# Ordering a weight copy behind the middle of an earlier weight slab, in a two-layer hybrid decoder kernel

## The chip, the core and the metric

The kernel runs on one core of one Trainium2 chip. The core has a matrix engine (TensorE, PE in the profile, with its weight loads as PEld), VectorE (DVE), ScalarE (ACT), GpSimd (POOL) and SyncE (SP, which here only issues transfers). Each engine takes its instructions from its own queue, in order. The metric is the device time of one execution in microseconds (us); the median of the runs counts.

## The reference

The reference computes two identical decoder layers on 512 tokens of width 1024, in float32. Each layer adds a block of four causal token mixers and then a SwiGLU feed-forward block:

```python
u = h @ w_in                       # one projection for all mixers and gates
y_a, y_b, y_c, y_d = fox(u), gla(u), retention(u), ssd(u)
merged = (g[:, :, 0] * (y_a @ w_up_a) + g[:, :, 1] * (y_b @ w_up_b)
          + g[:, :, 2] * (y_c @ w_up_c) + g[:, :, 3] * (y_d @ w_up_d))
x = x + merged @ w_out             # h = rms_norm(x, ln1)
gate, up = jnp.split(rms_norm(x, ln2) @ w_ffn_in, 2, axis=-1)
x = x + (jax.nn.silu(gate) * up) @ w_ffn_out    # 2816 hidden columns
```

Nearly all the arithmetic is in the products with weights. The weights are read once.

## The kernel before, in words

**Weights as slabs.** Every weight matrix is cut into blocks of 128 x 128. The order in which the program uses the blocks is written into the list `keys`, and eight blocks in a row make a slab (`SLAB = 8`, a tile of 128 x 1024 float32, 512 KB). There are 218 slabs in this stream, 109 per layer. `load()` (lines 247 to 253) allocates a raw tile `wr` (two buffers) and issues its transfer on SP's queue (line 252).

**High and low parts.** To keep float32 accuracy, each operand is split into a high part in the format float32r and the rest. `convert()` (lines 259 to 267) calls `split()` for a slab: line 214 is a ScalarE copy that writes the high part `wh`, and line 215 is a VectorE subtraction that writes the low part `wl`. Both have three buffers (the pool `wp`). A block times an activation tile is three matmuls, all issued in `mm` at line 200: high by high, high by low, low by high (`mm3`). So a usual slab is 24 matmuls of 512 columns. When the subtraction is done the raw tile is free and the next load into it can go.

**Who asks for a slab.** `block()` (lines 275 to 286) hands out one block after another. When it crosses into a slab it calls `ahead()`, which loads and converts up to `AHEAD = 2` slabs, so the conversion of slab n is written in the program at the first block of slab n-1. `wide()` (lines 288 to 297) hands out three slabs per layer in another shape and doesn't go through `block()`.

**Who sets the order.** The program is traced in this order, and a list scheduler with a timeline simulation then writes each engine's queue. It may move an instruction ahead of others when the simulated operands and buffers are there. Between engines there are semaphores for real dependences: a copy into `wh` waits for the transfer of `wr`, and for the last matmul of the slab that had the buffer before, which is slab n-3. `order(a, b)` (lines 226 and 227) adds an edge of class NoSync from instruction a to instruction b. Before the change its only use is in `act()`, where it keeps the loads of activation tables in their order on ScalarE.

**The stages of a layer.** First the projections with the mixers between them (`proj`, `group`; the mixers are generators, and weight products from the list `fill` are put between their steps), then `w_out` (lines 1207 to 1210), then the feed-forward block. This has a plain group of two hidden blocks and then four parts (`PARTS = (6, 6, 6, 4)`). In each part, `run()` computes hidden blocks with a Strassen scheme on its own stream of weights (`wsq`, loaded at lines 1274 and 1288 into `rq`, `wr` and `wl`, with high parts at lines 1295 and 214), and then the product with `w_ffn_out` takes slabs from the main stream: six per part, four in the last. Four output blocks are computed as a group, the others one by one, and each result is scaled and added to x on VectorE (lines 1424 and 1425). The loads of the Strassen stream share the two `wr` buffers and SP's queue with the slabs.

Of the kernel before, what the change touches and what calls it, by code (L numbers as in the profile page):

```python
# [35 lines left out]
SLAB = 8  # L36
# [98 lines left out]
def trunk(ctx: ExitStack, tc: tile.TileContext, keys, qkeys, xin, pos, wst, wsq, par, ext, cst, out):  # L135
    nc = tc.nc
    V, A, G, T = nc.vector, nc.scalar, nc.gpsimd, nc.tensor
# [20 lines left out]
    def piece(tag, shift=0):  # L158
        t = wp.tile([P, SLAB * P + 64], F32R, tag=tag, name=nm(tag))
        return t[:, shift:shift + SLAB * P]  # L160
# [36 lines left out]
        return ap.rearrange("p (c t) -> p c t", c=n)  # L197

    def mm(o, l, r, start, stop):
        T.matmul(o, lhsT=l, rhs=r, start=start, stop=stop, skip_group_check=True)  # L200

    def mm3(o, l, r, start, stop):
        (lh, ll), (rh, rl) = l, r
        mm(o, lh, rh, start, False)
        mm(o, lh, rl, False, False)
        mm(o, ll, rh, False, stop)
# [4 lines left out]
            mm(o, a, b, start and i == 0, stop and i == 1)  # L211

    def split(src, hi, lo):
        A.copy(out=hi, in_=src)  # L214
        V.tensor_tensor(out=lo, in0=src, in1=hi.bitcast(F32), op=ALU.subtract)  # L215
        return hi, lo

    def split_tile(t):
        return split(t, TT(F32R), TT(F32R))

    def split_small(t, shape, tag):
        return split(t, sp.tile(shape, F32R, tag=tag + "h", name=nm(tag), bufs=1), sp.tile(shape, F32R, tag=tag + "l", name=nm(tag), bufs=1))

    seen = {"set": None, "last": None}

    def order(a, b):
        tc.add_manual_dep(a.ins, b.ins.name, mybir.DependencyInfo(mybir.DependencyClass.NoSync, mybir.DependencyReason.DATA), reason="table")
# [13 lines left out]
            seen["last"] = i  # L241
        return i

    raw, ready = [], []
    cap = [SLABS]

    def load():
# [7 lines left out]
    def halves(n):  # L255
        w = SLAB * P
        return [slice(0, w // 2), slice(w // 2, w)] if n < 2 else [slice(0, w)]

    def convert():
        n = len(ready)  # L260
        if n < SLABS:
            far = n % (BLOCKS // SLAB) in TOKEN
            hi, lo = (piece("wh", 16), piece("wl", 48)) if far else (piece("wh"), piece("wl"))
            for h in halves(n):
                split(raw[n][:, h], hi[:, h], lo[:, h])
            ready.append((hi, lo))
            raw[n] = None

    def ahead(n):
        while len(ready) < min(SLABS, cap[0], n):  # L270
            if len(raw) == len(ready):
                load()
            convert()

    def block(*key, width=1):
        n = len(keys)
        if n % SLAB == 0:
            ahead(n // SLAB + AHEAD)
            if n // SLAB:
                ready[n // SLAB - 1] = None  # L280
        for i in range(width):
            keys.append(key[:-1] + (key[-1] + i * P,))
        i = n % SLAB
        hi, lo = ready[n // SLAB]
        sl = slice(i * P, (i + width) * P)
        return hi[:, sl], lo[:, sl]
# [141 lines left out]
    def group(name, l, cols, src, nk, hook=None):  # L428
        ps = [MX() for _ in cols]
        for k in range(nk):  # L430
            if hook and k == 4:
                hook()
            for i, c in enumerate(cols):
                mm3(ps[i], block(name, l, k, c), src[k], k == 0, k == nk - 1)
        return ps

    def proj(name, l, c, src, nk):
        ps = MM()
        for k in range(nk):
            mm3(ps, block(name, l, k, c), src[k], k == 0, k == nk - 1)  # L440
        return ps

    def layer(l, n1, scope):
# [72 lines left out]
        def tokmajor(dst, c, stacked=False):  # L516
            st = {}

            def go(half):
                def f():  # L520
                    if half == 0:
                        if not stacked:
                            dst.append(vp.tile([P, NB, 256], F32, tag="v", name=nm("v")))
                        st["ps"] = [MM(), MM()]
                    for k in range(4 * half, 4 * half + 4):
                        w = block("w_in", l, k, c, width=2)
                        assert (len(keys) - 1) // SLAB % (BLOCKS // SLAB) in TOKEN
                        for tb in range(NB):
                            ts = slice(tb * P, (tb + 1) * P)
                            o = st["ps"][tb // 2][:, (tb % 2) * 256:(tb % 2) * 256 + 256]  # L530
                            mm3(o, (n1.hi[:, k, ts], n1.lo[:, k, ts]), w, k == 0 and tb % 2 == 0, k == KD - 1)
                    if half:
                        for tb in range(NB):
                            v, rt = st["ps"][tb // 2][:, (tb % 2) * 256:(tb % 2) * 256 + 256], n1.rt[:, tb:tb + 1]
                            if stacked:
                                t = TT(F32R).rearrange("p (h s d) -> p h s d", h=NH, s=2)
                                v = v.rearrange("p (h d) -> p h d", h=NH)
                                act(out=t[:, :, 0], in_=v, func=AF.Copy, scale=rt)
                                V.scalar_tensor_tensor(out=t[:, :, 1], in0=v, scalar=rt, in1=t[:, :, 0].bitcast(F32), op0=ALU.mult, op1=ALU.subtract)
                                dst.append(t)  # L540
                            else:
                                act(out=dst[0][:, tb], in_=v, func=AF.Copy, scale=rt)
                return f
            return [(4.1, go(0)), (4.1, go(1))]
# [906 lines left out]
    o, w = PAR_OFF["ln1"]  # L1451
# [78 lines left out]
```

## Time and profile before

| What | Value |
|---|---|
| Runs | 1712.86, 1713.11 and 2853.69 us, median 1713.11 |
| The profiled execution's own time | 1713.04 us |
| Its span, first to last instruction | 1711.3 us |
| Granted TensorE clock | 1.000 |
| Busy: PE, PEld, DVE, ACT, POOL | 99%, 87%, 71%, 50%, 13% |
| Read from HBM, written | 191.28 MB, 2.10 MB |

The profile is a recording of one execution. Of a group of instructions it gives the line, the engine, the operation, the tiles written and read (without their numbers), the shapes and the count; after the bar stand the busy time and the mean of one in ns, and then the idle time of the engine just before them with what ended it. A row of the timeline is: start, length, engine, line, operation, tiles, shapes, count, and in brackets the idle time before it and what ended that. A row of the waits is: engine and line that waited, for whom, microseconds in total, times, the longest. A piece of the chain is: start, length, engine, tiles and line, count. `PE mm L200` is a matmul into a PSUM tile named mm, `mx` one of the other four PSUM banks. The ends of matmuls are modelled and overlap the next start, so their pace is read from starts.

### The profile page before, as it was taken

To read this page: it belongs to the slowest core of one execution; us is meant where nothing else is said; L and a number is where in the kernel's file an instruction comes from. 1 tells how busy PE (TensorE), PEld (TensorE's weight loads), DVE (VectorE), ACT (ScalarE), POOL (GpSimd) and SP (SyncE) were. 2 spreads that over 40 slices of the span, in tenths; PEclk is the share of its full clock that TensorE was granted. 3 is DMA by queue.
4 is the path that set the end of the run, shared out by engine and by line. 5 is a ranking of instruction groups with operands and counts; after the bars stand their busy time and mean duration, and the time that the engine had idled before them with its cause. 6 is when DMAs were issued, how large, how long until landed. Compare 5 with 4: busy or idle time off the path is not lost.

```text
span 1711.3 us, 25115 instructions
## 1 busy us (share of the span) xinstructions
PE 1700.9 (99%) x10124; PEld 1480.5 (87%) x10124; DVE 1210.9 (71%) x1693; ACT 863.5 (50%) x1194; POOL 216.4 (13%) x221
## 2 busy tenths in 40 slices
PE   9999999999999999999999999999999999999998
PEld 7878888888888999998988788888888889999997
DVE  6867666768677677675777666767776677767666
ACT  5425543546347646464544354435554474655643
POOL 3021210022101010101020212200221010101010
PEclk9999999999999999999999999999999999999999
DMA  5322222222235657575333222222222265665653
GB/s 200 106 74 74 75 86 75 86 87 74 85 110 142 194 132 188 136 185 120 91 98 111 74 74 74 87 76 94 77 87 87 99 171 163 153 174 139 177 115 106
DMA packets 54693, 195.00 MB, mean 114 GB/s; under 512 B 6064, under 2 KB 6448, under 8 KB 54576
## 3 DMA queue, kind: packets, MB, share of 16 engines
q1 hardware_dynamic: 45072, 160.45, 29.0%
q0 software_dynamic: 8640, 31.46, 10.3%
q8 instruction: 79, 1.29, 0.3%
q10 hardware_dynamic: 864, 1.48, 0.2%
q14 instruction: 38, 0.31, 0.1%
HBM read 191.28 MB, written 2.10 MB: 113 GB/s over the span
## 4 chain that ended last, share of the span: by engine, by line
PE 97%; DVE 1%; DMA 1%; ACT 1%; issue 0%; SPq 0%; DVEq 0%
PE mm L200 65%; PE mx L200 31%; PE mx L1080 1%; DMA x<-in_x_dram 0%; DMA wr<-in_wst_dram 0%; ACT wh L214 0%; DVE wl L215 0%; PE mx L693 0%; DVE t L371 0%; ACT L233 0%; ACT g L238 0%; DVE t L1169 0%; PE mx L952 0%; PE mx L872 0%; DVE n L409 0%
## 5 line engine op out<-in xcount | busy, mean ns | idle before, releaser
L214 ACT CAST wh<-wr 128x1024 fp32r<-128x1024 f32 (+1 forms) x240 | 250.1, 1043 | 367.8 <-PE mm L200 224.8
L200 PE MATMUL mm<-xh,wh 128*128 128x512 f32 (+1 forms) x1184 | 428.5, 362 | 0.9 <-DVE t L1169 0.9
L200 PE MATMUL mm<-xh,wl 128*128 128x512 f32 (+1 forms) x1184 | 427.9, 361 | 0.0
L200 PE MATMUL mm<-xl,wh 128*128 128x512 f32 (+1 forms) x1184 | 427.3, 361 | 0.0
L215 DVE TENSOR_TENSOR wl<-wr,wh 128x1024 fp32r<-128x1024 f32 (+1 forms) x220 | 285.5, 1299 | 118.4 <-ACT wh L214 116.0
L200 PEld LDWEIGHTS mm<-xh,wh 128*128 128x128 f32 x1184 | 222.4, 188 | 35.1 <-DVE t L1169 1.8
L200 PEld LDWEIGHTS mm<-xh,wl 128*128 128x128 f32 x1184 | 222.5, 188 | 34.6 <-issue 1.3
L200 PEld LDWEIGHTS mm<-xl,wh 128*128 128x128 f32 x1184 | 222.4, 188 | 33.9 <-issue 1.3
L200 PE MATMUL mm<-t,wh 128*128 128x512 f32 x448 | 140.2, 392 | 0.0
L200 PE MATMUL mx<-xl,wh 128*128 128x256 f32 (+1 forms) x448 | 138.3, 309 | 0.0
L200 PE MATMUL mx<-xh,wh 128*128 128x256 f32 (+1 forms) x448 | 136.0, 311 | 2.2 <-ACT wh L214 2.2
L1288 POOL DMA_DIRECT2D wl<-in_wsq_dram x60 | 51.9, 865 | 517.7 <-ACT wl L1287 368.1
L200 PE MATMUL mx<-f,wh 128*128 128x512 f32 x352 | 108.2, 390 | 0.0
L200 PE MATMUL mm<-f,wh 128*128 128x512 f32 x352 | 105.9, 389 | 0.0
L200 PEld LDWEIGHTS mm<-t,wh 128*128 128x128 f32 x448 | 83.2, 188 | 17.1
L215 DVE TENSOR_TENSOR l<-rq,wh 128x1024 fp32r<-128x1024 f32 x60 | 73.2, 1220 | 33.1 <-ACT wh L214 18.7
L200 PEld LDWEIGHTS mx<-xh,wh 128*128 128x128 f32 x448 | 84.0, 188 | 8.5 <-ACT wh L214 3.3
L200 PE MATMUL mx<-xh,wl 128*128 128x256 f32 (+1 forms) x288 | 91.0, 327 | 0.0
L200 PEld LDWEIGHTS mx<-xl,wh 128*128 128x128 f32 x448 | 84.1, 188 | 5.1
L200 PE MATMUL mm<-t,wl 128*128 128x512 f32 x224 | 87.4, 390 | 0.0
L214 ACT CAST wh<-rq 128x1024 fp32r<-128x1024 f32 x60 | 63.0, 1050 | 43.8 <-PE mm L200 21.5
L200 PEld LDWEIGHTS mm<-f,wh 128*128 128x128 f32 x352 | 66.1, 188 | 13.5
(280 smaller groups left out, 3438.1 us busy)
## 6 DMA issues: line engine op xcount, KB each, us to landing
wr<-in_wst_dram SPq DMA_DIRECT2D x216, 512.0 KB, 3.5
rq<-in_wsq_dram SPq DMA_DIRECT2D x60, 512.0 KB, 5.5
wl<-in_wsq_dram POOLq DMA_DIRECT2D x60, 512.0 KB, 7.3
wr<-in_wsq_dram SPq DMA_DIRECT2D x20, 512.0 KB, 6.9
out_dram<-x SPq DMA_DIRECT2D x8, 256.0 KB, 2.0
x<-in_x_dram SPq DMA_DIRECT2D x3, 512.0 KB, 6.5
wr<-in_wst_dram SPq DMA_DIRECT2D x4, 256.0 KB, 5.5
x<-in_x_dram SPq DMA_DIRECT2D x2, 256.0 KB, 4.6
```

The lines of the kernel that those rows point to most:

```text
L200: T.matmul(o, lhsT=l, rhs=r, start=start, stop=stop, skip_group_check=True)
L214: A.copy(out=hi, in_=src)
L215: V.tensor_tensor(out=lo, in0=src, in1=hi.bitcast(F32), op=ALU.subtract)
L1080: T.transpose(ps[:, W:W + P], zs[qb][:, kb * P:(kb + 1) * P], ident)
L1288: G.dma_start(out=lo, in_=wsq[j], accum_op=ALU.add)
```

## The change

`mm` and `split` now remember the last matmul and the last high-part copy that were traced. When `block()` hands out the fifth block of a slab (`i == SLAB // 2`), the last matmul traced before it, the third of the fourth block, is kept as that slab's middle. After each `split` in `convert()`, if slab n-2 has a middle, the copy of slab n gets an edge to it by `order()`.

```diff
     def mm(o, l, r, start, stop):
-        T.matmul(o, lhsT=l, rhs=r, start=start, stop=stop, skip_group_check=True)
+        seen["mm"] = T.matmul(o, lhsT=l, rhs=r, start=start, stop=stop, skip_group_check=True)
...
     def split(src, hi, lo):
-        A.copy(out=hi, in_=src)
+        seen["copy"] = A.copy(out=hi, in_=src)
...
-    raw, ready = [], []
+    raw, ready, middle = [], [], {}
...
                 split(raw[n][:, h], hi[:, h], lo[:, h])
+                if n - 2 in middle:
+                    order(seen["copy"], middle[n - 2])
...
         i = n % SLAB
+        if i == SLAB // 2:
+            middle[n // SLAB] = seen["mm"]
         hi, lo = ready[n // SLAB]
```

No operand, shape, buffer or transfer changes.

## The prediction

> **What bounds the kernel now.** I read the page first, then whom TensorE (PE) waited for, then the chain of work that ended last, for PE's pace, then the waits and the timeline of ScalarE (ACT), on which the changed instruction runs.
>
> ```profile
> span 1711.3 us, 25115 instructions
> ...
> PE 1700.9 (99%) x10124; PEld 1480.5 (87%) x10124; DVE 1210.9 (71%) x1693; ACT 863.5 (50%) x1194; POOL 216.4 (13%) x221
> ```
> ```profile
> PE mx L200 <- ACT wh L214: 2.2, 3, 1.1
> PE mm L200 <- POOL t L327: 1.4, 1, 1.4
> PE mx L200 <- DVE t L215: 1.2, 2, 0.7
> PE mm L200 <- DVE t L1169: 0.9, 2, 0.5
> ```
>
> PE is busy for 1700.9 of 1711.3 us, and all recorded waits of PE come to 2.2 + 1.4 + 1.2 + 0.9 = 5.7 us. Of these the first two rows belong to the start (warm-up, and the first three slabs); in the middle of the kernel PE waits 2.1 us in all. No other engine's idle time can be worth more than this, so a gain has a floor close by. A loss has none.
>
> Busy records overlap, so a busy PE could still be a slow one. Its pace is in the pieces of the chain (start, length, what):
>
> ```profile
> 503.10 21.76 PE mm L200 x96
> 585.92 16.34 PE mx L200 x72
> 602.27 19.12 PE mm L200 x96
> 621.39 2.72 PE mx L200 x24
> 1434.47 16.34 PE mx L200 x72
> 1450.82 19.12 PE mm L200 x96
> 1469.94 2.72 PE mx L200 x24
> ```
>
> In the first row 96 matmuls of 512 columns, which are four slabs, take 21.76 us: 226.7 ns each, 5.44 us for a slab of 24, 2.72 us for half a slab.
>
> **What the change does, part by part.** It adds no instruction and no byte. It adds an ordering edge from the ScalarE copy of slab n's high part (line 214, called by convert) to the last matmul before the fifth block of slab n-2. The edge is of class NoSync: I take it as an order for the list scheduler that writes the queues, without a semaphore, so on the chip the copy still waits only for its load and for its buffer. What changes is where it stands in ScalarE's queue. In the code 210 of 218 slabs get an edge: not the first two, and not the slab two behind each of the six that wide() consumes, since those never pass through block().
>
> (1) The copy. Its rows on the page, and ScalarE's own waits:
>
> ```profile
> L214 ACT CAST wh<-wr 128x1024 fp32r<-128x1024 f32 (+1 forms) x240 | 250.1, 1043 | 367.8 <-PE mm L200 224.8
> ...
> L215 DVE TENSOR_TENSOR wl<-wr,wh 128x1024 fp32r<-128x1024 f32 (+1 forms) x220 | 285.5, 1299 | 118.4 <-ACT wh L214 116.0
> ```
> ```profile
> ACT wh L214 <- PE mm L200: 246.3, 95, 7.5
> ```
> ```profile
> 519.23 1.06 ACT L214 CAST wh<-wr 128x1024 fp32r<-128x1024 f32 x1 [3.24 <-PE mm L200]
> ```
>
> In this row of the steady stage a copy has stood at the head of ScalarE's queue for 3.24 us, until a matmul freed its buffer. There are three buffers, so that matmul was the last of slab n-3: the copy starts as slab n-2 begins, and slab n begins two slabs later: 2 x 5.44 = 10.88 us, less 1.05 for the copy, leaves 9.83 us of cover. Half a slab later 9.83 - 2.72 = 7.11 us are left. Cost on PE: 0, hidden by the one and a half slabs of matmuls still to run. Without that cover each late microsecond would be one of PE.
>
> What stands behind the copy goes up to 2.72 us sooner, and the 246.3 us in 95 waits (2.6 us each, near the 2.72 that the copy moves) should fall by more than half. I value this at 0, because PE waits 2.2 us for that engine, at the start. Its upper bound is the 2.1 us of waits in mid-kernel.
>
> (2) The subtraction behind it (line 215 on VectorE, 1.30 us mean) moves as far: 9.83 - 1.30 = 8.53 us of cover become 5.81. In VectorE's queue it stood with 116.0 us of waits for the copy; behind it stand PSUM evacuations, for which PE waited 0.9 us in all.
>
> (3) The loads. SP's queue holds the load of slab n+2 behind that subtraction:
>
> ```profile
> SPq L252 <- DVE wl L215: 954.1, 176, 12.1
> ```
> ```profile
> wr<-in_wst_dram SPq DMA_DIRECT2D x216, 512.0 KB, 3.5
> ```
>
> Copy 1.05, subtraction 1.30 and landing 3.5 make 5.85 us from one copy to the data of the copy two slabs on, against 10.88 us: 5 us to spare, unchanged, since both ends move together. Cost 0. The Strassen loads (line 1274) that share SP's queue come at most 2.72 us later. POOL's queue isn't passed.
>
> (4) The ends of the feed-forward parts, the tightest place. There the raw buffers are shared with Strassen tiles, and the sixth slab of a part can be loaded only when the fifth's subtraction is done. The layers are copies of the same work, and their ScalarE rows differ:
>
> ```profile
> 587.06 1.05 ACT L214 CAST wh<-wr 128x1024 fp32r<-128x1024 f32 x1 [1.37 <-DMA wr<-in_wst_dram]
> ...
> 597.83 1.03 ACT L214 CAST wh<-wr 128x1024 fp32r<-128x1024 f32 x1
> 607.97 1.05 ACT L214 CAST wh<-wr 128x1024 fp32r<-128x1024 f32 x1 [9.11 <-DMA wr<-in_wst_dram]
> ```
> ```profile
> 1437.69 1.05 ACT L214 CAST wh<-wr 128x1024 fp32r<-128x1024 f32 x1 [3.19 <-DMA wr<-in_wst_dram]
> ...
> 1448.12 1.05 ACT L214 CAST wh<-wr 128x1024 fp32r<-128x1024 f32 x1 [1.64 <-DMA wr<-in_wst_dram]
> 1456.74 1.05 ACT L214 CAST wh<-wr 128x1024 fp32r<-128x1024 f32 x1 [7.57 <-DMA wr<-in_wst_dram]
> ```
>
> The second layer runs 1434.47 - 585.92 = 848.55 us behind. Less that, these copies start at 589.14, 599.57 and 608.19: 2.08, 1.74 and 0.22 us later than in the first layer. PE's pieces there are the same to 0.01 us (16.34, 19.12, 2.72). So the kernel has already run copies two microseconds later, nearly the size of this change, in its tightest stretch, at no cost. I take 0 here; what would cost is in the rivals, at most 6 x 0.8 = 4.8 us.
>
> (5) The last part of each layer. Its fourth slab is copied early, and its first four matmuls fill PE before the middle of the second slab:
>
> ```profile
> 841.86 1.06 ACT L214 CAST wh<-wr 128x1024 fp32r<-128x1024 f32 x1
> ```
> ```profile
> 845.51 1.52 PE L200 MATMUL mm<-f,wh 128*128 128x512 f32 x6
> ...
> 848.46 0.39 PE L200 MATMUL mx<-f,wl 128*128 128x512 f32 x1
> ```
>
> The last four of those six are that slab's; the matmul at 848.46 is the one its copy is to follow. They must go behind it in the program. If nothing fills their place PE loses 4 x 0.2267 = 0.9 us in each layer, 1.8 in both; if the second slab's own matmuls move up, nothing. I take 0, since their order alone changes.
>
> (6) The start. PE waited 1.05 us for the third slab's copy, which stood behind a square that was itself waiting:
>
> ```profile
> 18.74 0.63 ACT L238 ACTIVATE n<-x 128x512 f32<-128x512 f32 x1 [1.05 <-DVE n L409]
> 19.28 1.03 ACT L214 CAST wh<-wr 128x1024 fp32r<-128x1024 f32 x1
> ```
>
> Ahead of that square the copy would gain up to 1.05 us, behind one more it would lose 0.63. The first slab's middle is past by then, so I take 0.
>
> The sum is 0. The profiled execution took 1713.04 us (span 1711.3 and 1.7 around it), 0.07 below the median of the runs shown, so I predict **1713.0 us**. The bounds are -2.1 - 1.05 = -3.2 and 4.8 + 1.8 + 0.6 = +7.2: 1709.8 to 1720.2.
>
> **Rivals.** (a) The edge does nothing on the chip, because the copies are held by the buffer or the load wherever they stand; or the edge becomes a wait. Either way one and a half slabs of cover remain: 1713.0. For it speaks that waits for loads also hold copies; against it the 95 waits for PE, which show copies queued too early.
>
> (b) ScalarE's freed time is what PE's remaining waits hang on. They vanish: 1713.0 - 2.1 - 1.05 = 1709.9. Against it: they name VectorE, not ScalarE.
>
> (c) Slower, by the chain in (4). Its link after the copy:
>
> ```profile
> 603.35 1.22 DVE L215 TENSOR_TENSOR wl<-wr,wh 128x1024 fp32r<-128x1024 f32 x1
> ...
> 607.11 0.69 DVE L1425 TENSOR_TENSOR x<-x,f 128x512 f32<-128x512 f32 x1
> ```
> ```profile
> 612.99 1.07 PE L200 MATMUL mm<-f,wh 128*128 128x512 f32 x4
> ```
>
> The subtraction ends at 604.57 and lets the last slab's load go; that slab's copy (607.97, above) ends at 609.02 and PE needs it at 612.99, 3.97 us later. If the late copy lets the subtraction slip behind the next evacuation pair, which ends at 607.80, it ends at 609.02 instead of 604.57, 4.45 us late. The high part is then 0.5 us late, the low part (needed after four matmuls, at 613.90, ready at 609.02 + 1.23 + 4.45 = 614.70) 0.8 us. Three parts in two layers: 6 x 0.8 = 4.8, so 1717.8 us. It decides from a slip of 3.97 us. One pair further (one more block column of 18 matmuls, 4.1 us) adds 4.1 x 6: 1742, and a second one passes 2%.
>
> (d) PE's pace isn't its floor, and the copies slow it. The pieces speak against it: the same counts take the same time to 0.01 us with the copies two microseconds apart. If it were so, a few per cent of 1700.9 could go: 3% would be 51 us, 1662.
>
> [...]
>
> **Chances.** Forecast 0.67; (a) 0.08; (b) 0.10; (c) 0.14, of which 0.02 is beyond 2%; (d) 0.01. The forecast's bounds already hold (a), (b) and the first form of (c), so the range is these bounds, rounded out by about a microsecond for small matmuls that may stand in another order: 1708 to 1721. Faster by over 2% (34 us, about what a measurement of this kernel can tell from no change) is (d) alone, 0.01; slower by over 2% 0.02; within 2% 0.97.
>
> **What would show it.** Right: the row of ScalarE's waits for PE before wh falls from 246.3 us to under 125; copies in the steady stage start two to three microseconds after the slab boundary and no longer with a wait of 3.24 us; PE's waits stay under 7 us; the pieces of 21.76, 16.34 and 19.12 us are there unchanged. Wrong: PE waiting for wh or wl outside the first 21 us, most of all at the end of a feed-forward part (c), or in the last part of a layer (5); or equal PE waits and shorter pieces (d).

## The result, and the profile after

The changed kernel took 1742.49 us in the median (1741.01 to 1743.47), the kernel before 1712.86 us: a ratio of 1.0171 with a 95% interval of 1.016 to 1.0182. The ratio leaves out the one run of 2853.69 us of the kernel before. The forecast was 1713.0 us in a range of 1708 to 1721. The kernel is 29.6 us slower, and the prediction was wrong.

The profiled execution of the changed kernel took 1741.01 us. First its page, the span and the engines' busy time:

```profile
span 1739.3 us, 25088 instructions
...
PE 1713.5 (99%) x10124; PEld 1485.0 (85%) x10124; DVE 1208.7 (69%) x1693; ACT 861.3 (50%) x1194; POOL 215.1 (12%) x221
```

The span is 28.0 us longer. PE does the same 10124 matmuls and is 12.6 us longer busy, so less than half of the loss can be slower matmuls; the rest is idle time. Whom PE waited for, in the changed kernel (total, times, longest):

```profile
PE mm L200 <- DVE wl L215: 5.6, 2, 2.8
PE mm L200 <- ACT wh L214: 4.2, 4, 1.9
PE mx L1084 <- DVE t L1075: 3.6, 2, 1.8
PE mx L200 <- ACT t L214: 2.0, 4, 0.6
PE mx L200 <- DVE t L215: 1.6, 6, 0.3
PE mx L200 <- ACT wh L214: 1.5, 2, 1.2
PE mm L200 <- POOL t L331: 1.4, 1, 1.4
PE mm L200 <- DVE t L1173: 0.9, 2, 0.5
```

These come to 20.8 us where it was 5.7. Now a usual matmul waits for `wl` and for `wh`, twice or four times in the whole kernel, so once or twice in each layer. The prediction named just this sign as the one that would prove it wrong.

The new waits stand in two short stretches of each layer, both among the mixers. The stretches of the first layer, in the table of windows of the changed kernel (PE, PEld, DVE, ACT and POOL busy, then the granted clock, the DMA share and GB/s):

```profile
225.00:243.00 18.00, 18.00 (x81) 14.71 (x79) 14.35 (x19) 10.26 (x13) 2.27 (x2) 1.00 0.09 30
243.00:250.00 7.00, 3.29 (x10) 1.68 (x10) 6.05 (x10) 2.80 (x4) 4.04 (x3) 0.98 0.01 2
250.00:256.00 6.00, 6.00 (x21) 4.76 (x21) 6.00 (x5) 1.05 (x1) 3.83 (x2) 0.74 0.51 175
...
394.00:398.00 4.00, 2.08 (x7) 1.26 (x7) 1.75 (x3) 3.97 (x5) 1.18 (x2) 0.50 0.02 4
```

PE is full up to 243 us. Then it is busy for 3.29 of 7 us, and behind that the granted clock falls: 0.74 over the next six microseconds, with one stretch at half speed. At 394 us the whole window runs at 0.50. Over the span the mean granted clock is 0.994, which is about 0.006 x 1739.3 = 10.4 us of lost matmul time; before it was 1.000. So the 28.0 us are 20.8 - 5.7 = 15.1 us of waits, some 10.4 us of half clock behind the waits, and about 2.5 us that these two views don't give.

**The first place.** ScalarE in the changed kernel (the row of 1.99 us is the copies of slabs 37 and 38):

```profile
232.58 0.62 ACT L214 CAST t<-t 128x512 fp32r<-128x512 f32 x1 [2.50 <-DVE t L644]
237.65 2.19 ACT L214 CAST t<-t 128x512 fp32r<-128x512 f32 x4 [4.45 <-DVE t L644]
240.08 1.92 ACT L238 ACTIVATE g<-g 128x2048 f32<-128x2048 f32 x1 [0.25 <-DVE g L1159]
242.00 1.28 ACT L233 ACT_TABLE_LOAD   x1
243.30 0.62 ACT L214 CAST t<-t 128x512 fp32r<-128x512 f32 x1
243.82 1.99 ACT L214 CAST wh<-wr 128x1024 fp32r<-128x1024 f32 x2
```

The same two copies in the kernel before:

```profile
231.65 1.06 ACT L214 CAST wh<-wr 128x1024 fp32r<-128x1024 f32 x1 [0.89 <-PE mm L200]
233.62 0.63 ACT L214 CAST t<-t 128x512 fp32r<-128x512 f32 x1 [0.92 <-DVE t L640]
237.09 1.06 ACT L214 CAST wh<-wr 128x1024 fp32r<-128x1024 f32 x1 [2.84 <-PE mm L200]
```

Slab 37's copy starts 12.2 us later, not 2.7. It now stands behind five casts (a group norm's result, `t`, and rotary operands), the sigmoid of a gate, a table load and one more cast. Those wait themselves: 2.50 and 4.45 us for VectorE's chain of the norm, and the sigmoid 0.25 us for VectorE's evacuation of a gate column. The low part, in VectorE's timeline, first after, then before:

```profile
245.16 2.47 DVE L930 TENSOR_TENSOR t<-mx,sinT 128x512 f32<-128x512 f32 x4
247.56 0.67 DVE L1173 TENSOR_TENSOR t<-mm,g 128x512 f32<-128x512 f32 x1
248.16 1.21 DVE L215 TENSOR_TENSOR wl<-wr,wh 128x1024 fp32r<-128x1024 f32 x1
```
```profile
233.44 1.22 DVE L215 TENSOR_TENSOR wl<-wr,wh 128x1024 fp32r<-128x1024 f32 x1
```

The subtraction moved by 14.7 us, more than the copy: the copy ended at about 244.9, and the subtraction still waited behind four rotary multiplications and an evacuation. PE there, in the changed kernel:

```profile
249.42 0.56 PE L200 MATMUL mm<-xh,wl 128*128 128x512 f32 x1 [2.81 <-DVE wl L215]
249.78 0.63 PE L200 MATMUL mm<-xh,wh 128*128 128x512 f32 x1
250.20 0.63 PE L200 MATMUL mm<-xl,wh 128*128 128x512 f32 x1
```

PE begins slab 37, has used the high part and waits 2.81 us for the low part. From 249.78 to 250.20 is 0.42 us, where matmuls of this shape start 0.2267 us apart at a granted clock of 1.00 (96 in 21.76 us, before): the granted clock is 0.50 there, for 3.41 us from 249.71 on.

**Which matmul the edge names.** Where this copy was to stand was read wrongly ahead of the run. `seen["mm"]` is the last matmul that was traced, whatever it belongs to. It is the third matmul of the slab's fourth block only if nothing was traced between the fourth and the fifth. Slab 35's fifth block is the first of a new product, for a gate column, and between two products `drain()` steps a mixer; here that is `ret()`, which has just traced its eight rotary matmuls (`mx<-t,cr`). So the edge for slab 37 names the last of these and not the middle of slab 35. In the kernel before it ran at 253.54, 21.9 us behind the copy that was now to follow it; first before, then after:

```profile
253.54 0.40 PE L200 MATMUL mx<-t,cr 128*128 128x512 f32 x1
```
```profile
244.70 0.50 PE L200 MATMUL mx<-t,cr 128*128 128x512 f32 x1 [0.23 <-DVE t L215]
```

The scheduler put the copy behind the casts that these matmuls need, and all eight of them (241.88 to 244.70) ahead of slab 37 in PE's order, where before they stood among the matmuls of slab 38 (249.13 to 253.54). Going through `kernel.py` in the order in which it traces its matmuls gives every such edge. Of the 210 edges 196 name a matmul of their own slab, and 14, seven in each layer, one of a mixer:

| Edge at | Copies whose edge names a mixer's matmul, per layer |
|---|---|
| 2nd block | none |
| 3rd block | 53, 57, 63, 68 |
| 5th block (the change) | 35, 37, 54, 58, 59, 64, 69 |
| 7th block | 55, 60, 65, 70 |

**The second place** is the softmax of another mixer, around slabs 58 to 60. ScalarE in the changed kernel, with the copy of slab 58 at 381.58 and those of 59 and 60 at 395.86:

```profile
374.13 0.72 ACT L238 ACTIVATE t<-t,fmx 128x512 f32<-128x512 f32 x1 [7.42 <-DVE fmx L1071]
...
380.73 0.97 ACT L214 CAST t<-mx 128x512 fp32r<-128x512 f32 x2 [5.40 <-PE mx L1084]
381.58 1.06 ACT L214 CAST wh<-wr 128x1024 fp32r<-128x1024 f32 x1
...
395.86 1.99 ACT L214 CAST wh<-wr 128x1024 fp32r<-128x1024 f32 x2
```
```profile
393.95 0.45 PE L1084 MATMUL mx<-cs,t 128*128 128x128 f32 x1 [1.83 <-DVE t L1075]
396.95 0.80 PE L200 MATMUL mm<-xh,wh 128*128 128x512 f32 x1 [1.92 <-ACT wh L214]
```

In the kernel before:

```profile
368.56 0.72 ACT L238 ACTIVATE t<-t,fmx 128x512 f32<-128x512 f32 x1 [5.66 <-DVE fmx L1067]
...
369.75 1.05 ACT L214 CAST wh<-wr 128x1024 fp32r<-128x1024 f32 x1
375.18 0.59 ACT L214 CAST t<-mx 128x512 fp32r<-128x512 f32 x1 [4.38 <-PE mx L1080]
```

Before, slab 59's copy ran at 369.75, between the exponential that waits for `fmx` and the cast that waits for `mx`. Now both, and more, stand ahead of it: 26.1 us later, of which 5.9 are the lag that the first place left behind. Here PE waits 1.92 us for the high part itself. It is done with slab 58 at 389.8 and takes up slab 59 at 396.95; between them it has only matmuls of the softmax, waits 0.57 and 1.83 us for operands of these, and then for the copy. So 2.4 us of the waits here are put down to the softmax, but the wait that ends last is for the weights.

**Where nothing happened.** The steady stage, ScalarE after, with the copy that ran at 519.23 before:

```profile
532.89 1.06 ACT L214 CAST wh<-wr 128x1024 fp32r<-128x1024 f32 x1 [3.24 <-PE mm L200]
```

This copy still stands at the head of the queue for 3.24 us and starts as its buffer comes free, the very number of before. Counted in the two written queues, leaving out table loads and other slab copies, 168 of the 218 copies have as many ScalarE instructions ahead of them as before; two have one or two fewer, and 48 have 1 to 11 more. Those with four or more are, in each layer, 37, 38, 58 to 62, 64 and 65: four of the seven slabs of the table, and copies close behind them. ScalarE's waits changed as little:

```profile
ACT wh L214 <- PE mm L200: 212.4, 80, 6.7
```

And the ends of the feed-forward parts, in the chain of work of the changed kernel:

```profile
599.39 16.34 PE mx L200 x72
615.74 19.12 PE mm L200 x96
634.86 2.72 PE mx L200 x24
```

The same three pieces as before, with the same lengths.

### The profile page after: what moved, and what is told of

It is laid out like the page before. It is cut to its first block, busy times and chain, and to the rows that moved or that the text cites. A ratio compares the mean times of both kernels' runs of the same rounds, so it can differ in the third digit from the quotient of the medians.

```text
span 1739.3 us, 25088 instructions
## 1 busy us (share of the span) xinstructions
PE 1713.5 (99%) x10124; PEld 1485.0 (85%) x10124; DVE 1208.7 (69%) x1693; ACT 861.3 (50%) x1194; POOL 215.1 (12%) x221
## 4 chain that ended last, share of the span: by engine, by line
PE 96%; ACT 2%; DVE 1%; issue 1%; DMA 0%; ACTq 0%; DVEq 0%
PE mm L200 65%; PE mx L200 30%; ACT L233 1%; PE mx L1084 0%; DVE wl L215 0%; DVE t L215 0%; ACT wh L214 0%; DVE t L1173 0%; ACT g L238 0%; DMA x<-in_x_dram 0%; PE mx L697 0%; ACT t L214 0%; ACT n L238 0%; DVE t L375 0%; ACT xh L238 0%
## 5 line engine op out<-in xcount | busy, mean ns | idle before, releaser
L215 DVE TENSOR_TENSOR wl<-wr,wh 128x1024 fp32r<-128x1024 f32 (+1 forms) x220 | 280.8, 1279 | 117.9 <-ACT wh L214 115.3
L200 PEld LDWEIGHTS mm<-t,wh 128*128 128x128 f32 x448 | 83.5, 189 | 17.9 <-ACT wh L214 0.9
```

The source lines that it names most:

```text
L200: seen["mm"] = T.matmul(o, lhsT=l, rhs=r, start=start, stop=stop, skip_group_check=True)
```

## The experiments

Three theories. **Q, the queue:** the edge moves a copy by whole places in ScalarE's in-order queue; a copy that lands behind instructions which wait for a mixer's chain is late by those waits, and costs as soon as that is more than its cover of about 10 us. **H, half a slab:** all copies have lost half a slab of cover each, and the loss grows with how late the edge is and with how many copies have it. **O, PE's order:** the edge changes the order of PE's own matmuls, and that costs. Slab numbers are those of a layer (37 is 37 and 146 of the stream).

| Run | Edge | Median, us | Ratio to before, 95% |
|---|---|---|---|
| e1_off_at_five | all but 37, 38, 58, 59, 60 | 1722.80 | 1.0054 (1.0039 to 1.0069) |
| e2_only_five | those five alone | 1743.87 | 1.0178 (1.0163 to 1.0194) |
| e3_only_37 | 37 alone | 1727.46 | 1.0085 (1.007 to 1.01) |
| e4_only_58_60 | 58, 59, 60 alone | 1731.04 | 1.0105 (1.0088 to 1.0121) |
| e5_off_at_six | all but those five and 64 | 1711.72 | 0.9993 (0.9984 to 1.0002) |
| e6_behind_cast | 37, behind a cast, not a matmul | 1722.48 | 1.0056 (1.0041 to 1.0071) |
| e7_second_block | all, at the 2nd block | 1712.43 | 0.9997 (0.9987 to 1.0007) |
| e8_third_block | all, at the 3rd block | 1713.98 | 1.0005 (0.9996 to 1.0015) |
| e9_casts_on_vector | 37, norm's casts on VectorE | 1726.53 | 1.008 (1.0063 to 1.0097) |
| e10_sigmoid_behind | 37, sigmoid behind the copy | 1727.61 | 1.0085 (1.007 to 1.01) |
| e11_seventh_block | all, at the 7th block | 1720.95 | 1.0044 (1.0029 to 1.0059) |
| e12_low_part_first | 37, subtraction put first | 1717.96 | 1.0029 (1.0018 to 1.004) |

### Which edges cost

e1_off_at_five takes the edges of the five suspected slabs away from the changed kernel:

```diff
-                if n - 2 in middle:
+                if n - 2 in middle and n % (BLOCKS // SLAB) not in (37, 38, 58, 59, 60):
```

> The changed kernel without the edge for five of the 109 slabs of each layer (numbers 37, 38, 58, 59 and 60 of the layer); the other 200 edges stay. Theory Q (queue jump: the edge costs only where it lets the copy fall behind ScalarE instructions that wait for the mixers' own chains; the loss sits at two places of each layer): 1713 to 1718 us, no half-speed clock in mid-kernel, PE waits for wh and wl there under 1 us. Rival H (every copy loses half a slab of cover, a little everywhere): 200 of 210 edges are left, so about 1741 us. Rival O (the scheduler's new order of the mixers' matmuls costs the time, whichever edge triggers it): anything between, with long PE waits on other tiles than wh and wl.

Measured: 1722.80 us, 9.6 us over before: 20 of the 30 us are gone with ten of 210 edges, but the rest was more than expected. Its trace names one slab more. ScalarE, with the copies of slabs 64 and 65 (64's was at 401.77 before), and PE's waits:

```profile
412.26 2.00 ACT L214 CAST wh<-wr 128x1024 fp32r<-128x1024 f32 x2
```
```profile
PE mm L200 <- DVE wl L215: 5.5, 2, 2.7
```

In the changed kernel the copy of slab 64 came at 422.9 us, but PE was itself 14 us behind by then, and no wait showed.

e2_only_five is the complement, the kernel before with edges for these five alone:

```diff
-                if n - 2 in middle:
+                if n - 2 in middle and n % (BLOCKS // SLAB) in (37, 38, 58, 59, 60):
```

> The kernel before with the edge for those five slabs of each layer alone, ten edges. Theory Q: the whole loss, 1739 to 1744 us, with the clock at half speed twice in each layer. Rival H: 10 of 210 edges, so 1713 to 1715 us.

Measured: 1743.87 us. Ten edges make the whole loss.

e3_only_37 and e4_only_58_60 split them (`== 37` and `in (58, 59, 60)` in the same condition).

> The kernel before with one edge per layer, for slab 37. Theory Q: both slabs 37 and 38 fall behind the last casts of one mixer and the first of the next, as in the changed kernel, for two edges: 6 to 7 us per layer, so 1725 to 1727 us. Rival H: two edges, at most 2 x 2.7 us if nothing covered them, 1713 to 1718 us.

> The kernel before with the edge for slabs 58, 59 and 60 of each layer alone. Theory Q: the second place alone, 7.5 to 8.5 us per layer by the lag read in the trace of the changed kernel, so 1728 to 1730 us; with the run with slab 37 alone it adds up to the whole loss. Rival H: 1713 to 1714 us.

Measured: 1727.46 and 1731.04 us, 14.3 and 17.9 us over before, together 32.1 where the five made 30.7. The two places nearly add up, and a single edge per layer costs 14 us.

e5_off_at_six leaves out slab 64 as well.

```diff
-                if n - 2 in middle:
+                if n - 2 in middle and n % (BLOCKS // SLAB) not in (37, 38, 58, 59, 60, 64):
```

> The first run left out five edges per layer and still lost 9.6 us, all of it, by its trace, at slab 64, whose copy stood behind eight instructions of ScalarE more than before. Here the edge for slab 64 is left out too; 198 of 210 edges stay. Theory Q: 1712 to 1715 us, no half-speed clock in mid-kernel. Rival H: 198 edges, 1740 us. If a further place opens as slab 64 did, 1716 to 1725 us.

Measured: 1711.72 us, 1.2 us under before on the same chip, ratio 0.9993 (0.9984 to 1.0002). Of the 198 edges left, 192 name a matmul in the middle of their own slab, and together they cost nothing. H falls: it is not the half slab. The other six (slabs 35, 54 and 69 of each layer) name a mixer's matmul, but their copies have kept their place or gone back by one or two, and they cost nothing either. Of all versions this has the lowest median, but its interval touches 1.

### How late the edge is

e7_second_block and e8_third_block move every edge forward, e11_seventh_block back:

```diff
-        if i == SLAB // 2:
+        if i == 1:
```

(and `i == 2`, `i == 6`).

> The changed kernel with the edge to the last matmul before the second block of slab n-2 instead of the fifth: an eighth of a slab, 0.7 us, after the buffer is free. Theory Q: the queue is that of the kernel before but for one to three small moves, none behind a waiting chain: 1712.5 to 1714 us. Rival H (loss in proportion to the lateness, 29.5 us at four eighths): 7 us, 1720 us.

> The edge to the last matmul before the third block: a quarter of a slab, 1.4 us. Slab 37 keeps its place, slabs 53 to 63 of each layer fall behind four to eight instructions. Theory Q: a loss at one place per layer, 5 to 12 us each, so 1723 to 1737 us, slab 37 undisturbed. Rival H: half of 29.5 us, spread, 1728 us.

> The changed kernel with the edge to the middle moved on from the fifth block to the seventh. By the theory that lost cover is what costs, the loss grows beyond that of the fifth block: over 1743 us, 1757 if in proportion. By the theory of ScalarE's queue the time goes by which copies stand behind waiting instructions: in this order slab 37 isn't moved at all, slabs 55 and 60 are moved by 9 and 10 instructions, so the waits of 2.8 us at slab 37 are gone, and the time lies between 1714 and 1735 us, below that of the fifth block although the edge is later.

Measured: 1712.43, 1713.98 and 1720.95 us, beside 1742.49 at the fifth block. A later edge costs less, so cost does not follow lateness. It goes better with what the edges name: at the second block none names a mixer's matmul, and nothing is lost. The third block was a miss for both theories as they were written: its copies do go back by up to eight places, but without loss. Its ScalarE, with the copies of slabs 57 and 58, which were at 358.8 and 361.84 before:

```profile
370.26 2.01 ACT L214 CAST wh<-wr 128x1024 fp32r<-128x1024 f32 x2
```

They are 11.5 and 9.4 us late, the first of them behind an exponential that itself waited 8.24 us, and still no usual matmul waited for `wh` or `wl`. At the seventh block slab 37 isn't moved at all, and the loss is at slab 55, whose edge names a softmax matmul and which went back by nine places. There PE waited 2.4 us in each layer for a cast of the softmax (`t`), in a stretch from 355.66 us on in which it had nothing but softmax matmuls; it took up slab 55 at 360.57, just as that slab's copy (359.49, 1.05 us) was done. Whether an edge costs is decided slab by slab.

### Which queue it is

e6_behind_cast has no edge to a matmul. In the kernel before, slab 37's copy is ordered behind the last cast of the rotary step, on ScalarE itself:

```diff
-        A.copy(out=hi, in_=src)
+        seen["copy"] = A.copy(out=hi, in_=src)
...
                 split(raw[n][:, h], hi[:, h], lo[:, h])
+                if n % (BLOCKS // SLAB) == 37:
+                    order(seen["copy"], seen["turn"])
...
             sr = [split_tile(t) for t in rq + rk]
+            seen["turn"] = seen["copy"]
```

> The kernel before with no edge to any matmul: the copy of slab 37 of each layer is ordered behind the last ScalarE cast of the rotary step of the retention mixer, an edge within ScalarE. Theory Q (position in ScalarE's queue is all that counts): the same time as with the edge for slab 37 to the matmul, 1726 to 1729 us, copies of slabs 37 and 38 about 12 us late. Rival O (what the matmul edge does to the scheduling of PE): 1713 us.

Measured: 1722.48 us, outside both expectations. ScalarE's queue is the same as in e3, and the copy as late (244.42 us). That cast writes an operand of the very rotary matmuls that the edge of e3 names, so the two edges ask for nearly the same. The loss comes without any edge to PE, but O does not fall by this: PE's order is that of e3, with the eight rotary matmuls ahead of slab 37. The loss is 9.6 us, not 14.3, and the one difference at the place is VectorE's order, where the subtraction stood one multiplication and one evacuation further forward. The subtraction, which now holds PE for 1.6 us:

```profile
247.55 1.22 DVE L215 TENSOR_TENSOR wl<-wr,wh 128x1024 fp32r<-128x1024 f32 x1
```

Two runs asked which of the instructions ahead of the copy holds it. e9_casts_on_vector is e3 with the norm's casts on VectorE; e10_sigmoid_behind is e3 with the sigmoid ordered behind the copy.

```diff
-                res[j] = split_tile(t)
+                hi, lo = TT(F32R), TT(F32R)
+                V.tensor_copy(out=hi, in_=t)
+                V.tensor_tensor(out=lo, in0=t, in1=hi.bitcast(F32), op=ALU.subtract)
+                res[j] = (hi, lo)
```
```diff
                     order(seen["copy"], middle[n - 2])
+                    seen["slab"] = seen["copy"]
...
-                        act(out=st["t"], in_=st["t"], func=AF.Sigmoid)
+                        a = act(out=st["t"], in_=st["t"], func=AF.Sigmoid)
+                        if (len(ready) - 1) % (BLOCKS // SLAB) == 37:
+                            order(a, seen["slab"])
```

> The kernel with the edge for slab 37 alone, and the two casts of the group norm's result (the ones for which ScalarE waited 2.85 and 4.45 us ahead of that slab's copy) made by VectorE instead. If these waiting casts are what holds the copy, they are gone from its queue, the copy comes 2 to 3 us sooner than at 244.4 us, and the time falls from 1727.5 to between 1713 and 1718 us. If it is held by the sigmoid behind them, which waits for PE's last matmul of a gate column (it started at 240.64 us) and is followed by a table load of 1.28 us, then the copy still starts at 244 to 245 us, PE still waits 2 to 3 us for the low part, and the time stays between 1723 and 1730 us.

> The kernel with the edge for slab 37 alone, and a second edge that puts the sigmoid behind that slab's copy, so that the copy stands behind six casts and nothing else. If the sigmoid and the table load (1.92 and 1.28 us) are what makes the copy too late, it starts at 241 to 242 us instead of 244.4, PE's 3.7 us of waits at the place shrink to 1.5 us or less, no half clock follows, and the time is 1713 to 1718 us. If what costs is the edge to the matmul, or the copy's being late at all (it is still 9 to 10 us later than in the kernel before), the time stays between 1723 and 1730 us.

Measured: 1726.53 and 1727.61 us. In e9 the casts that waited are gone and nothing is won: the copy starts at 244.75, behind the sigmoid. In e10 it came 2.3 us sooner, as expected, and nothing was won either: a miss. Its ScalarE, VectorE and PE:

```profile
242.10 1.05 ACT L214 CAST wh<-wr 128x1024 fp32r<-128x1024 f32 x1
```
```profile
249.65 1.21 DVE L215 TENSOR_TENSOR wl<-wr,wh 128x1024 fp32r<-128x1024 f32 x1
```
```profile
250.91 0.80 PE L200 MATMUL mm<-xh,wl 128*128 128x512 f32 x1 [3.31 <-DVE wl L215]
```

The copy ends at 243.15 and its subtraction starts at 249.65. Q, as a theory of ScalarE's queue alone, falls here: at slab 37 VectorE's queue came last. So the theory was changed, to two queues: the edge moves the copy in ScalarE's queue, the subtraction moves with it in VectorE's, each behind whatever stands there, and PE waits for the later of the two. e12_low_part_first tests it: e3, with the four rotary multiplications ordered behind the subtraction. ScalarE's queue is unchanged.

```diff
                     order(seen["copy"], middle[n - 2])
+                    seen["slab"] = seen["low"]
...
-                V.tensor_tensor(out=u, in0=ps, in1=sinT, op=ALU.mult)
+                a = V.tensor_tensor(out=u, in0=ps, in1=sinT, op=ALU.mult)
+                order(a, seen["slab"])
```

(`seen["low"]` is the last subtraction of `split`.)

> The kernel with the edge for slab 37 alone, and a second edge that puts the four rotary multiplications on VectorE behind that slab's subtraction. ScalarE's queue stays as it was, so the copy still starts at 244 to 245 us, some 12.7 us late. If the place of the subtraction in VectorE's queue decides (there it stood behind four multiplications, 2.47 us, and an evacuation, 0.68 us, and started at 248.70 us), it starts at 245.4 to 246 us, PE's wait of 2.81 us for the low part falls to 0.5 us or less, no half clock follows, and the time is 1713 to 1718 us. If the copy's place in ScalarE's queue alone decides, nothing changes and the time is between 1724 and 1730 us.

Measured: 1717.96 us. ScalarE and VectorE:

```profile
244.80 1.99 ACT L214 CAST wh<-wr 128x1024 fp32r<-128x1024 f32 x2
```
```profile
246.13 1.72 DVE L215 TENSOR_TENSOR wl<-wr,wh 128x1024 fp32r<-128x1024 f32 x1
```

The copy is as late as ever, PE's order from 222 to 250 us is that of e3, PE's longest wait for `wl` is 0.3 us, and two thirds of the loss are gone. So, with the copy as late and PE in the same order, these two thirds hang on the subtraction's place. The four runs beside each other:

| Run | Copy starts | Subtraction starts | PE's longest wait for `wl` | Over before |
|---|---|---|---|---|
| e10 | 242.10 | 249.65 | 3.3 | 14.5 |
| e3 | 244.38 | 248.70 | 2.8 | 14.3 |
| e6 | 244.42 | 247.55 | 1.6 | 9.6 |
| e12 | 244.80 | 246.13 | 0.3 | 4.8 |

The loss goes with the subtraction and not with the copy, which in e10 is the earliest of the four (PE comes to the place 0.5 to 0.9 us later in e10 than in the others, mostly from a wait at its start). The 4.8 us left in e12 are short waits at the same place (for `wh`, for `wl`, and for rotary operands from ScalarE and VectorE, which PE's new order asks for sooner; 0.2 to 0.5 us each), in part; the rest wasn't traced.

## Why the prediction was wrong, point by point

**The step that failed is (1)**: "on the chip the copy still waits only for its load and for its buffer", from which the copy was moved by at most 2.72 us and given 7.11 us of cover. The edge has no semaphore, and that was right: slab 37's copy starts at 243.82, ahead of the matmul at 244.70 that its edge names. Two things were not. The copy also waits for what stands ahead of it in ScalarE's queue, and the edge chose that: eight more instructions at slab 37. And the 2.72 us took every edge to name the middle of slab n-2. For 14 of the 210 it names a mixer's matmul instead, at slab 37 one that ran 21.9 us behind the copy, so the copy had to go behind the work of the mixer that this matmul needs. The copy moved by 12.2 us there, and by 20 to 26 at slabs 58 to 60 (14 to 20 without the lag of the first place), against the 9.83 us of cover that the steady stage showed. Of most copies the opposite is true: they didn't move at all, and ScalarE's waits for PE went from 246.3 to 212.4 us, not below 125. The step took the steady stage, whose queue holds little beside the copies, for the whole kernel. Its rows were true and came from the one kind of stage in which the edge does nothing. In the trace of the changed kernel the 1162 instructions written for ScalarE and the 1693 for VectorE start in the very order of the two written queues, and slab 37's copy, with eight more ahead of it, 12.2 us behind its old place.

**(2)** failed with it: the subtraction didn't move "as far" but by 14.7 us, since it has a queue of its own. Rival (c) had this mechanism, a subtraction that slips behind other work of VectorE, at the wrong place: it was sought at the ends of the feed-forward parts, where every piece of the chain kept its length. That its second price, 1742, is near the measured time is chance; it was made of six places of which none moved.

**(3)** held: no load is among PE's waits. **(4)** held, 16.34, 19.12 and 2.72 us as before. **(5)** held: in the last part of the first layer four matmuls change places, and the lag behind the kernel before is 13.59 us ahead of it and 13.59 at its end. **(6)** held within 0.3 us. Rival (a) was right for most edges and wrong for the kernel; (b) had the sign wrong. For (d) nothing new came: the pace of the undisturbed pieces is unchanged.

**A cost that was in no step** is the clock. PE's waits of 15.1 us were made dearer by some 10.4 us at half clock. The prediction priced a late operand by its lateness alone.

What stays open: no run gave slab 37 an edge to the third matmul of slab 35's own fourth block, so that this would be free is argued, from the 192 such edges of e5. At the second place no run tells ScalarE's queue, VectorE's queue and PE's new order apart; only the wait that ends last points to the copy. Why the copies of slabs 35, 54 and 69 hardly moved, though their edges name mixers' matmuls too, wasn't looked into. And about 2.5 us of the 28.0 are not accounted for.

## What to carry to other kernels

Before pricing an edge, look up which instruction it names: "the last one traced" can belong to other work, and then the edge carries all that this work waits for. An edge without a semaphore wasn't a small delay here: it moved slab 37's copy by eight places and 12.2 us in ScalarE's queue, and the subtraction that depends on it by 14.7 us in VectorE's. So read from the trace, stage by stage, what stands in both queues behind the old place and what that waits for, above all where chains of other work cross the same engine. The matmul engine's own order moved as well, by eight rotary matmuls. The cover of 9.83 us, measured in the regular stage, said little of the irregular ones: at slab 37, with the copy 12.2 us late and the subtraction 14.7, PE waited 2.81 us; with the copies of e8 11.5 and 9.4 us late no usual matmul waited; and over the four runs at slab 37 the price went with the later of the two queues. Where the matmul engine runs dry, look for the clock behind it as well: here it made some 10.4 us beside 15.1 us of waits.

## What the runs showed of the hardware

A few short waits stand right ahead of the half clock. In the changed kernel no wait at the first place was longer than 2.81 us, PE was busy for 3.29 of the 7 us from 243 on, and from 249.78 on matmuls start 0.42 us apart instead of 0.2267, at a granted clock of 0.50. Nor did the same wait always have it behind it. In e1_off_at_five slab 64 waits alike in both layers (PE's waits for `wl` are 5.5 us in two, the longest 2.7); its windows, first of layer 1, then of layer 2:

```profile
415.48:418.89 3.41, 1.75 (x9) 1.14 (x8) 3.41 (x6) 2.60 (x4) 2.87 (x4) 1.00 0.00 0
418.89:422.31 3.42, 2.34 (x10) 1.96 (x11) 3.42 (x6) 3.12 (x3) 1.18 (x1) 1.00 0.37 92
1268.87:1272.28 3.41, 0.67 (x3) 0.23 (x3) 3.41 (x5) 3.38 (x4) 3.11 (x4) 1.00 0.00 0
1272.28:1275.69 3.41, 3.41 (x9) 2.62 (x9) 3.04 (x9) 2.48 (x5) 0.00 (x0) 0.50 0.73 209
```

In the first layer the clock stays at 1.00, in the second it is 0.50 for 3.41 us, which is 1.7 us of lost time.

In the changed kernel the half-speed stretches before the last matmuls start at 249.71, 393.07, 1113.28 and 1256.64 us and last 3.41, 6.83, 3.41 and 6.83 us. The later three start 143.36, 863.57 and 1006.93 us behind the first, which are 42, 253 and 295 steps of 3.413 us, the length of the short ones. Cut into cells of this length, with a border at 249.71, the trace reads as follows. The cells just ahead of the four stretches have PE busy for 18%, 55%, 34% and 40%, and the first halves of the two long stretches for 32% and 42%. Every other cell from 21 us to the last matmuls has 65% or more, and none of these has half clock behind it. In e1_off_at_five the windows above are such cells, cut from the start of its stretch at 1272.28. In layer 1 the waits are spread over neighbouring cells, and PE is busy for 51% and 68% of them; in layer 2 one cell gets most of them, PE is busy for 20% of it, and the half clock follows. So the 51% had no half clock behind it where the 55% of the changed kernel had: the busy share of a cell alone doesn't settle it, and what sets the clock isn't shown by these runs. What they show is that the half clock went with how the waits fell on the cells, and not with the length of a single one: of two waits of 2.7 us, it came behind one.
